# Two rewrites in the delta stage of a hybrid decoder step: the 64-row blocks of a triangular inverse, and how the query norms are summed

## The chip, the cores and the metric

The kernel runs on one core of one Trainium2 chip. A core has five engines that run side by side and meet through semaphores: TensorE (PE in the profile, with its weight loads shown apart as PEld), VectorE (DVE), ScalarE (ACT), GpSimd (POOL) and SyncE (SP), which issues most of the DMAs. TensorE writes its products to PSUM, and the other engines copy them from there to SBUF. The metric is the device time of one launch in microseconds (us); lower is better. Three timed runs of the kernel before gave 2085.28, 2088.38 and 2094.0 us, the median being 2088.38 us.

## The reference, cut to what matters

The program is one inference step of one decoder layer for a prompt of 1024 tokens and eight single-token samples: a combined input projection, a gated DeltaNet branch, a sliding-window attention branch, their mixture, a convolutional feed-forward part, and a last RMSNorm. The change lies in the DeltaNet branch for the prompt, which has 8 heads of width 128. Cut to that branch, per head, the reference computes:

```
q, k, v = split(silu(conv4(z)))                     # 1024 x 128 each
q = q * rsqrt(sum(q*q, -1) + EPS) * 128**-0.5        # l2 norm of each query row
k = k * rsqrt(sum(k*k, -1) + EPS)
m = strict_lower(beta * k @ k.T * gam)               # per chunk of rows
t_inv = inverse(eye + m)                             # unit lower triangular
u, w = t_inv @ (v * beta), t_inv @ (k * beta * exp(decay))
# then a scan over the chunks with the carried state S:
v_new = u - w @ S
o = q_dec @ S + a_intra @ v_new
S = S * last + k_dec.T @ v_new
out = o * rsqrt(mean(o*o, -1) + EPS) * w_norm * silu(gate)
```

The kernel computes the same thing with chunks of 128 rows instead of 64, so each head has 8 chunks and each chunk has a 128x128 inverse.

## The kernel before, in words

The 1032 tokens lie along the free axis and the channels along the 128 partitions. Every projection is a product in three passes (the high and low parts of weights and activations, lines L180, L181 and L182), over 8 blocks of the contracted width, for three token parts of 384, 384 and 264 columns. These projections make up most of TensorE's work in every stage.

The delta stage works head by head. `delta_project` makes K, Q and V of a head (projection, short convolution, SiLU). `delta_prepare` (L866) makes what does not depend on the running state: it transposes K on TensorE (L190) in two groups of four chunks, takes the squares of each chunk's rows with a running sum on ScalarE (L888), and scales the transposed K into `kd` (L890). It does the same transposes and squares for Q, where only the sums `n2` are used: they join the epsilon in the output norm of the scan (L972). One addition (L892) then adds an epsilon to all sums of K and Q together; `nk`, `c1`, the products K K and K Q (L906, L907), `A` (L908) and `U` (L910) follow, then V's transposes (`vn`, L918), and two loads of a row of decays into the tile `ed`, with which Q is multiplied (L922, L923).

`unit_inverse` (L990) inverts the unit triangular 128x128 matrices of the head's 8 chunks, by blocks that double in size: 16-row blocks by substitution on VectorE (L1019, L1020), then 32-row blocks (L1038, L1044), then 64-row blocks (L1056, L1061), and at the end the 128-row matrix from its two 64-row halves. This last step has two products per chunk, of 64x64 by 64x64. The first (L1070) uses array rows 0 to 63 and writes to partitions 64 to 127, so it uses array columns 64 to 127; ScalarE copies all eight chunks' results to `Zb` (L1071). The second (L1074) uses array rows 64 to 127 and columns 0 to 63; ScalarE copies its results into the inverse `W` (L1075). Both results live in PSUM tiles with the tag `tp`, of which there are two, shared with `delta_prepare`.

`delta_scan` (L931 and on) then walks through the 8 chunks with the state S. Each chunk is a chain across three engines: K times S (L947, TensorE), y (L948, VectorE), W times y (L950, TensorE), s (L952, ScalarE), kd times s (L954, TensorE), the new S (L963, VectorE). Every fourth chunk takes squares of the outputs on ScalarE (L969).

The order of the work is made when the program is built. `weave` (L1258) gives each stream of a head a priority: inverse first, scan next, then the next head's preparation, while the projections of later heads and of the two branch gates (L1294 and L1295 finish the gates) have the lowest priority and are the filler. A scheduler then writes one fixed order for each engine. On the chip every engine runs its list in that order: an instruction that waits for a semaphore holds up all that stand behind it on its engine. `issue_after(x)` asks the scheduler to put what is written inside the block behind instruction `x`; it ties those instructions of the block that are on the same engine as `x`.

## Time and profile before

| what | value |
|---|---|
| timed runs | 2085.28, 2088.38, 2094.0 us (median 2088.38) |
| span of the profiled execution, first to last instruction | 2084.4 us |
| the profiled execution's own time | not given apart from its span; the fastest timed run is 0.9 us above that span |
| TensorE busy | 2012.7 us, 97% |
| VectorE busy | 1347.8 us, 65% |
| ScalarE busy | 900.2 us, 43% |
| GpSimd busy | 520.2 us, 25% |
| delta stage of the prompt, from the timeline | about 412 to 1105 us |

The profile's groups by line give busy time, the mean of one instruction in ns, and the idle time of the engine just before it. In the timeline a row gives the start, the length, the engine, the line, and how many such instructions follow each other. A TensorE instruction's length includes its way through the array, and the next one starts before it ends; so what an instruction costs TensorE is read from the distance between two starts. A full fp32 product of this kernel shows as two matmul instructions (two passes), a transpose as one, and a pass of a projection as one. "Window" means a stretch of time from the span's start.

### The profile page before, as it was taken

What the parts mean: (1) busy time and instruction counts of PE and PEld (TensorE: products, weight loads), DVE (VectorE), ACT (ScalarE), POOL (GpSimd) and SP (SyncE); (2) the same over time, 40 slices, a digit from 0 to 9 for tenths busy, and PEclk for the clock granted to TensorE, in tenths of its full rate; (3) what the DMA queues carried; (4) which work ended last, traced back from release to release, by engine and by line L of the source; (5) the groups of instructions that cost most, each with busy time, mean ns of one, the idle gap of its engine ahead of it and who ended that gap; (6) DMA issues with size and microseconds to landing.
All of it is one profiled execution on the core that took longest, in us unless ns stands there. A gap on an engine that the chain in (4) does not pass through costs nothing.

```text
span 2084.4 us, 41297 instructions
## 1 busy us (share of the span) xinstructions
PE 2012.7 (97%) x16245; PEld 1910.2 (92%) x16245; DVE 1347.8 (65%) x2714; ACT 900.2 (43%) x2233; POOL 520.2 (25%) x594
## 2 busy tenths in 40 slices
PE   7999998999999999989989999999999999999897
PEld 4987877799999999989989999999999999999897
DVE  5755768473655647656544675578876776767756
ACT  4664545433344243432342542354444444534443
POOL 2000000121321221201111000005575466446421
PEclk9999999999999999999999999999999999999999
DMA  8256443331332322312275855323333333488862
GB/s 300 62 144 210 135 167 116 117 94 51 80 80 61 73 72 52 89 42 62 63 223 172 285 186 163 112 63 97 105 91 112 102 92 112 136 305 266 291 215 94
DMA packets 301887, 275.75 MB, mean 132 GB/s; under 512 B 59730, under 2 KB 248111, under 8 KB 301676
## 3 DMA queue, kind: packets, MB, share of 16 engines
q1 hardware_dynamic: 295642, 252.14, 39.6%
q0 software_dynamic: 5552, 20.37, 2.8%
q8 instruction: 127, 2.08, 0.4%
q14 instruction: 68, 0.56, 0.1%
q10 hardware_dynamic: 498, 0.61, 0.1%
HBM read 212.93 MB, written 62.51 MB: 132 GB/s over the span
## 4 chain that ended last, share of the span: by engine, by line
PE 83%; DVE 5%; DMA 5%; ACT 3%; issue 1%; SPq 1%; POOL 1%; DVEq 0%; POOLq 0%; ACTq 0%
PE mm L180 19%; PE mm L181 18%; PE mm L182 18%; PE wv L180 3%; PE wv L182 3%; PE wv L181 3%; PE wy L182 2%; PE wy L180 2%; PE wy L181 2%; PE pv L652 1%; PE pt L190 1%; PE tp L190 1%; DVE x L1472 1%; PE mm L264 1%; PE rc L954 1%
## 5 line engine op out<-in xcount | busy, mean ns | idle before, releaser
L180 PE MATMUL mm<-b1h,wh 128*128 128x384 f32 (+1 forms) x1520 | 496.9, 328 | 3.7 <-ACT gt L1294 1.6
L181 PE MATMUL mm<-b1l,wh 128*128 128x384 f32 (+1 forms) x1520 | 489.3, 323 | 0.0
L182 PE MATMUL mm<-b1h,wl 128*128 128x384 f32 (+1 forms) x1520 | 488.0, 323 | 0.3 <-DVE wl L130 0.3
L180 PEld LDWEIGHTS mm<-b1h,wh 128*128 128x128 f32 x1520 | 286.7, 189 | 12.4 <-issue 4.6
L181 PEld LDWEIGHTS mm<-b1l,wh 128*128 128x128 f32 x1520 | 287.1, 189 | 4.4 <-issue 3.1
L182 PEld LDWEIGHTS mm<-b1h,wl 128*128 128x128 f32 x1520 | 286.3, 189 | 3.9 <-issue 2.8
L129 ACT ACTIVATE wh<-raw 128x1024 fp32r<-128x1024 f32 x83 | 87.0, 1049 | 122.4 <-PE mm L181 70.2
L130 DVE TENSOR_TENSOR wl<-raw,wh 128x1024 fp32r<-128x1024 f32 x82 | 101.0, 1233 | 57.2 <-ACT wh L129 55.1
L181 PE MATMUL mm<-pk,w 128*128 128x260 f32 (+1 forms) x440 | 124.8, 284 | 1.1 <-DVE pk L130 1.1
L180 PE MATMUL mm<-pk,w 128*128 128x260 f32 (+1 forms) x440 | 124.8, 284 | 0.0
L182 PE MATMUL mm<-pk,w 128*128 128x260 f32 (+1 forms) x440 | 124.5, 283 | 0.0
L130 DVE TENSOR_TENSOR w<-ws,w 128x512 fp32r<-128x512 f32 x88 | 78.0, 886 | 36.9 <-ACT w L129 36.7
L1626 ACT COPY bml<-mm 128x256 f32<-128x256 f32 (+1 forms) x132 | 48.9, 371 | 100.6 <-PE mm L182 96.7
L180 PE MATMUL mm<-bmh,w 128*128 128x260 f32 (+1 forms) x320 | 90.3, 282 | 0.0
L182 PE MATMUL mm<-bmh,w 128*128 128x260 f32 (+1 forms) x320 | 90.1, 282 | 0.0
L1681 DVE SCALAR_TENSOR_TENSOR fa<-fz,fcw,fa 128x512 f32<-128x512 f32 x88 | 75.2, 874 | 18.2 <-ACT fa L1679 17.9
L180 PE MATMUL mm<-b2h,wh 128*128 128x384 f32 (+1 forms) x256 | 83.2, 328 | 2.9 <-ACT wh L129 2.8
L181 PEld LDWEIGHTS mm<-pk,w 128*128 128x128 f32 x440 | 83.2, 189 | 1.3 <-DVE pk L130 1.3
L181 PE MATMUL mm<-b2l,wh 128*128 128x384 f32 (+1 forms) x256 | 83.6, 327 | 0.4 <-DVE b2l L130 0.4
L180 PEld LDWEIGHTS mm<-pk,w 128*128 128x128 f32 x440 | 83.2, 189 | 0.2 <-ACT bml L1626 0.2
L182 PEld LDWEIGHTS mm<-pk,w 128*128 128x128 f32 x440 | 83.4, 190 | 0.0
L182 PE MATMUL mm<-b2h,wl 128*128 128x384 f32 (+1 forms) x256 | 82.8, 326 | 0.0
(645 smaller groups left out, 5886.2 us busy)
## 6 DMA issues: line engine op xcount, KB each, us to landing
raw<-in_w_in_dram SPq DMA_DIRECT2D x59, 512.0 KB
ws<-in_w_ffn_down_dram SPq DMA_DIRECT2D x55, 256.0 KB
raw<-xd SPq DMA_DIRECT2D x47, 258.0 KB
raw<-in_w_ffn_down_dram SPq DMA_DIRECT2D x47, 256.0 KB
raw<-in_w_ffn_gate_dram SPq DMA_DIRECT2D x22, 512.0 KB
raw<-in_w_ffn_up_dram SPq DMA_DIRECT2D x22, 512.0 KB
qst<-in_w_mod_dram SPq DMA_DIRECT2D x16, 512.0 KB
raw<-in_w_mod_dram SPq DMA_DIRECT2D x16, 512.0 KB
```

What stands on the lines that cost most here:

```text
L129: self.nc.scalar.activation(hi, x, AF.Copy)
L130: (eng or self.nc.vector).tensor_tensor(lo, x, hi.bitcast(F32), op=ALU.subtract)
L180: mm(ps, whi, xhi, start=first, stop=False, **kw)
L181: mm(ps, whi, xlo, start=False, stop=False, **kw)
L182: self.last_mm = mm(ps, wlo, xhi, start=False, stop=last, **kw).ins
L190: self.nc.tensor.transpose(out, in_, self.ident[:p, :p])
L264: nc.tensor.matmul(ps[32 * j:32 * j + 32], self.cT[:, k0 + j, :], ws[j // 2][:, j % 2, :], start=k0 == 0, stop=k0 > 0)
L652: nc.tensor.matmul(pv[64 * r:64 * r + 64], V[:, n - back, ch], ps[:, r::2, :], start=back == 0, stop=back == (n > 0))
L954: yield step(nc.tensor.matmul(ds, kd[:, n, :], s, start=True, stop=True))
L1472: nc.vector.scalar_tensor_tensor(x[:, :np_], ps[:, :np_], by[:, j, 8:9], x[:, :np_], op0=ALU.mult, op1=ALU.add)
L1626: self.last_copy = nc.scalar.copy(r[p, i], x[p])
L1681: nc.vector.scalar_tensor_tensor(ai[:, c:e], zi[:, j + c:j + e], col(j), ai[:, c:e], op0=ALU.mult, op1=ALU.add)
```

## The change

The change edits two functions.

In `delta_prepare`, Q is no longer transposed. K's two groups stay as they were, and the epsilon is now added to K's sums alone. For Q, ScalarE squares four chunks in one instruction into a tile `q2` that shares the buffer of `ed`; four products with 32 columns of ones as the stationary operand then sum over the partitions, each for 32 of the 128 tokens of a chunk and into its own 32 partitions, so that the sums of token block j stand in partitions 32j to 32j+31. VectorE turns the 32x32 blocks (L899 of the changed kernel), after which the sum of each token stands in its own partition, and adds the epsilon (L900). `q2`'s two groups, like the two loads of decays behind them, use the one buffer of `ed`.

In `unit_inverse`, the two products of the 64-row halves are cut into groups of four chunks. The written loop has three rounds: the first product of chunks 0 to 3; the first product of chunks 4 to 7 in turn with the second product of chunks 0 to 3; the second product of chunks 4 to 7. Each of the copies to `Zb` and to `W` is split in two. The rounds behind the first are written inside `issue_after(copied)`, where `copied` is ScalarE's copy and the block holds TensorE instructions. In the changed kernel's line numbers the first product is L1084, the second L1086, and the copies are L1088 and L1090; the scan's lines have moved down by nine (L950 is L959, and so on).

```diff
-        for a, src in ((0, K), (1, Q)):
-            for c0 in (0, 4):
-                tp = self.t(psum, [P, 4, P], "tp", bufs=2)
-                for c in range(4):
-                    self.transpose(tp[:, c, :], src[:, c0 + c, :])
-                junk = self.t(pool, [P, P], "osq", bufs=1)
-                for c in range(4):
-                    nc.scalar.activation(junk, tp[:, c, :], AF.Square, accum_out=n2[:, a, c0 + c:c0 + c + 1])
-                if a == 0:
-                    nc.vector.tensor_tensor(kd[:, c0:c0 + 4, :], tp, bc(self.edd[:, h, c0:c0 + 4], 2, P), op=ALU.mult)
-                yield
-        nc.vector.tensor_scalar_add(n2, n2, 4 * EPS)
+        for c0 in (0, 4):
+            tp = self.t(psum, [P, 4, P], "tp", bufs=2)
+            for c in range(4):
+                self.transpose(tp[:, c, :], K[:, c0 + c, :])
+            junk = self.t(pool, [P, P], "osq", bufs=1)
+            for c in range(4):
+                nc.scalar.activation(junk, tp[:, c, :], AF.Square, accum_out=n2[:, 0, c0 + c:c0 + c + 1])
+            nc.vector.tensor_tensor(kd[:, c0:c0 + 4, :], tp, bc(self.edd[:, h, c0:c0 + 4], 2, P), op=ALU.mult)
+            yield
+        nc.vector.tensor_scalar_add(n2[:, 0], n2[:, 0], 4 * EPS)
+        for c0 in (0, 4):
+            q2 = self.t(pool, [P, 4, P], "ed", bufs=1)
+            nc.scalar.activation(q2, Q[:, c0:c0 + 4, :], AF.Square)
+            sums = self.t(psum, [P, 4, 32], "tp", bufs=2)
+            for j in range(4):
+                r = slice(32 * j, 32 * j + 32)
+                nc.tensor.matmul(sums[r], self.ones[:, 0:32], q2[:, :, r], start=True, stop=True)
+            turned = self.t(pool, [P, 4, 32], "osq", bufs=1)
+            nc.vector.transpose(turned.rearrange("p n i -> p (n i)"), sums.rearrange("p n i -> p (n i)"))
+            nc.vector.tensor_scalar_add(n2[:, 1, c0:c0 + 4], turned[:, :, 0], 4 * EPS)
+            yield
...
         zp = self.t(psum, [P, NCH, 2, 32], "tp", bufs=2)
-        for n in range(NCH):
-            nc.tensor.matmul(zp[64:128, n], U64[:, n, :], TT[0:64, :, n, :], start=True, stop=True)
-        nc.scalar.copy(Zb, zp[64:128].rearrange("p n a i -> p n (a i)"))
         qp = self.t(psum, [64, NCH, 64], "tp", bufs=2)
-        for n in range(NCH):
-            nc.tensor.matmul(qp[:, n, :], Zb[:, n, :], W[64:128, n, 64:128], start=True, stop=True)
-        nc.scalar.copy(W[0:64, :, 64:128], qp)
+        copied = None
+        for c0 in (0, 4, 8):
+            with self.tc.issue_after(copied) if copied else nullcontext():
+                for n in range(c0, c0 + 4):
+                    if n < NCH:
+                        nc.tensor.matmul(zp[64:128, n], U64[:, n, :], TT[0:64, :, n, :], start=True, stop=True)
+                    if c0:
+                        nc.tensor.matmul(qp[:, n - 4, :], Zb[:, n - 4, :], W[64:128, n - 4, 64:128], start=True, stop=True)
+            if c0 < NCH:
+                copied = nc.scalar.copy(Zb[:, c0:c0 + 4], zp[64:128, c0:c0 + 4].rearrange("p n a i -> p n (a i)")).ins
+            if c0:
+                nc.scalar.copy(W[0:64, c0 - 4:c0, 64:128], qp[:, c0 - 4:c0])
```

The change also moves instructions, since the scheduler writes the whole order anew. Three places show it. In the rows a semaphore's name tells whom an instruction waits for (`Activation` is ScalarE, `DVE` VectorE, `Pool` GpSimd, `DMAHW` a transfer).

First, TensorE in head 0, at the end of the inverse. Before, the second products stand as one block of eight behind a block of projections:

```order
L180 MATMUL mm_5421<-b1h_10_148,wh_5417 128x384
L181 MATMUL mm_5421<-b1l_11_149,wh_5417 128x384
L1074 MATMUL tp_5149<-W_4535,UZ_4957 64x64 [waits Activation_49]
L1074 MATMUL tp_5149<-W_4535,UZ_4957 64x64 x7
L190 MATMUL tp_5848<-ident,K_4654 128x128 [waits PE_49]
```

Now, in the same head, the first products of chunks 4 to 7 and the second products of chunks 0 to 3 stand in turn:

```order
L181 MATMUL mm_5423<-b1l_11_149,wh_5419 128x384
L1084 MATMUL tp_5139<-MR_5019,UZ_4957 64x64 [waits Activation_49]
L1086 MATMUL tp_5140<-W_4535,UZ_4957 64x64 [waits PE_49]
L1084 MATMUL tp_5139<-MR_5019,UZ_4957 64x64
L1086 MATMUL tp_5140<-W_4535,UZ_4957 64x64
L1084 MATMUL tp_5139<-MR_5019,UZ_4957 64x64
L1086 MATMUL tp_5140<-W_4535,UZ_4957 64x64
L1084 MATMUL tp_5139<-MR_5019,UZ_4957 64x64
L1086 MATMUL tp_5140<-W_4535,UZ_4957 64x64
L182 MATMUL mm_5423<-b1h_10_148,wl_5420 128x384
```

The two kinds of products alternate here; the remaining four second products stand 23 rows further down.

Second, TensorE in head 5. Before, the scan's last two chunks and the block of second products stand like this:

```order
L954 MATMUL rc_9735<-s_9733,kd_8864 128x128 [waits Activation_49]
L958 MATMUL o_9698<-s_9733,A_8916 128x128
L182 MATMUL mm_10286<-b1h_12_150,wl_10255 128x384
L947 MATMUL rc_9742<-S_9739,K_7325 128x128 [waits DVE_49]
L957 MATMUL o_9698<-S_9739,Q_7326 128x128
L950 MATMUL rc_9745<-y_9741,W_4535 128x128 [waits DVE_49]
L954 MATMUL rc_9749<-s_9747,kd_8864 128x128 [waits Activation_49]
L958 MATMUL o_9698<-s_9747,A_8916 128x128
L1074 MATMUL tp_10183<-W_4535,UZ_9991 64x64 [waits PE_49,Activation_49]
L1074 MATMUL tp_10183<-W_4535,UZ_9991 64x64 x7
L190 MATMUL tp_10876<-ident,K_9341 128x128 x4
```

Now the first product's second half has gone ahead of these rows, and the second product stands in two groups:

```order
L963 MATMUL rc_9745<-s_9743,kd_8872 128x128 [waits Activation_49]
L967 MATMUL o_9708<-s_9743,A_8924 128x128
L956 MATMUL rc_9752<-S_9749,K_7331 128x128 [waits DVE_49]
L966 MATMUL o_9708<-S_9749,Q_7332 128x128
L959 MATMUL rc_9755<-y_9751,W_4535 128x128 [waits DVE_49]
L963 MATMUL rc_9759<-s_9757,kd_8872 128x128 [waits Activation_49]
L967 MATMUL o_9708<-s_9757,A_8924 128x128
L1086 MATMUL tp_10184<-W_4535,UZ_10001 64x64 [waits PE_49,Activation_49]
L1086 MATMUL tp_10184<-W_4535,UZ_10001 64x64 x3
L190 MATMUL tp_10888<-ident,K_9351 128x128 x4
L1086 MATMUL tp_10184<-W_4535,UZ_10001 64x64 [waits Activation_49]
L1086 MATMUL tp_10184<-W_4535,UZ_10001 64x64 x3
```

The products do not alternate in this head, nor in any of heads 1 to 7: each of the two products stands as two groups of four, and each second group waits for ScalarE. The wait of a second group is for the copy of the first group of the same product (L1088 or L1090).

Third, ScalarE in head 5, around the copies of the first product. Before, the one copy stands ahead of the gate's tanh (L858) and of the two convolution rows (L791):

```order
L129 ACTIVATE wh_10350<-raw_10348 128x1024 [waits DMAHW3_49,PE_49]
L780 COPY z_9534<-mm_9594 128x264 [waits PE_49]
L1071 COPY UZ_9991<-tp_10173 64x512 [waits PE_49]
L952 ACTIVATE s_9733<-rc_9731,c_1414_8912 128x128 [waits PE_49,Activation_49]
L858 ACTIVATE th_10311<-mm_10286 128x384 [waits PE_49]
L791 ACTIVATE z_9534<-v_1476_9343 128x512 [waits DVE_49,Activation_49,Pool_49]
L791 ACTIVATE z_9534<-v_1476_9343 128x512 [waits Activation_49]
```

Now both copies stand behind them:

```order
L1072 COPY w_1625_10178<-tp_10143 32x256 [waits PE_49]
L858 ACTIVATE th_10323<-mm_10298 128x384 [waits PE_49]
L791 ACTIVATE z_9544<-v_1486_9353 128x512 [waits DVE_49,Pool_49]
L791 ACTIVATE z_9544<-v_1486_9353 128x512 [waits Activation_49]
L1088 COPY UZ_10001<-tp_10183 64x256 [waits PE_49]
L961 ACTIVATE s_9743<-rc_9741,c_1424_8920 128x128 [waits PE_49]
L1088 COPY UZ_10001<-tp_10183 64x256 [waits PE_49]
```

The tanh and the convolution rows have moved ahead of the copies, and the scan's s (L952, now L961) stands between the two halves.

## The prediction

> **What bounds the kernel now.** I read the page's busy times first, then the chain that ended last, then the delta stage in windows.

> ```profile
> span 2084.4 us, 41297 instructions
> PE 2012.7 (97%) x16245; PEld 1910.2 (92%) x16245; DVE 1347.8 (65%) x2714; ACT 900.2 (43%) x2233; POOL 520.2 (25%) x594
> PE 83%; DVE 5%; DMA 5%; ACT 3%; issue 1%; SPq 1%; POOL 1%; DVEq 0%; POOLq 0%; ACTq 0%
> ...
> 585.00:670.00 85.00, 84.70 (x754) 82.17 (x753) 50.30 (x109) 30.27 (x85) 14.62 (x23) 1.00 0.27 67
> ...
> 840.00:925.00 85.00, 78.56 (x699) 75.03 (x697) 51.90 (x111) 31.66 (x97) 14.57 (x21) 0.94 0.23 61
> 925.00:1005.00 80.00, 79.59 (x711) 77.12 (x710) 48.65 (x107) 27.61 (x76) 11.42 (x19) 0.99 0.25 66
> 1005.00:1070.00 65.00, 61.99 (x606) 57.59 (x605) 38.05 (x100) 28.19 (x90) 11.66 (x17) 1.00 0.36 101
> 1070.00:1130.00 60.00, 52.77 (x378) 50.69 (x377) 26.50 (x52) 16.35 (x43) 7.91 (x10) 0.97 0.77 223
> ```

> A window's row gives its length, then the busy time of TensorE, its weight loads, VectorE, ScalarE and GpSimd. TensorE is the bound, and the chain runs through it for 83% of the span. In a middle head (585 to 670) it is idle for 0.3 us: there only TensorE's own work counts, and work taken from ScalarE is worth nothing. From 840 on, where the projections that fill gaps run short, it is idle for 6.4 + 0.4 + 3.0 + 7.2 = 17.1 us: there the length of the chain across engines counts too. So each edit has two prices: TensorE time in all heads, and chain time in heads 5 to 7.

> **The change part by part.**

> *Query sums, on TensorE.* Four transposes leave, four products of two passes each come, 16 times (8 heads, two groups).

> ```profile
> 600.43 0.34 PE L182 MATMUL mm<-b1h,wl 128*128 128x384 f32 x1
> 600.61 0.60 PE L190 MATMUL tp<-ident,v 128*128 128x128 f32 x4
> 600.97 0.42 PE L180 MATMUL mm<-b1h,wh 128*128 128x384 f32 x1
> 601.22 0.33 PE L181 MATMUL mm<-b1l,wh 128*128 128x384 f32 x1
> ...
> 210.26 0.34 PE L180 MATMUL mm<-b1h,wh 128*128 128x384 f32 x1
> 210.53 0.62 PE L264 MATMUL mm<-wmh,cTr 128*32 128x512 f32 x2
> 210.98 0.60 PE L264 MATMUL mm<-wmh,cTr 128*32 128x512 f32 x2
> 211.41 1.04 PE L264 MATMUL mm<-raw,cTr 128*32 128x512 f32 x8
> 212.38 0.44 PE L181 MATMUL mm<-b1l,wh 128*128 128x384 f32 x1
> 212.66 0.34 PE L182 MATMUL mm<-b1h,wl 128*128 128x384 f32 x1
> ...
> 656.74 0.38 PE L947 MATMUL rc<-S,K 128*128 128x128 f32 x2
> 656.96 0.39 PE L957 MATMUL o<-S,Q 128*128 128x128 f32 x2
> ```

> A projection pass costs 0.18 (600.43 to 600.61). Four transposes hold the engine for 0.36, and the pass behind them takes 0.25 instead of 0.18: 0.43 us go per group. For what comes, the modulation's product L264 has the same form: 128 rows, a strip of 32 columns, four strips in turn. Its eight last passes of 512 columns take 0.97 (211.41 to 212.38), a round of four 0.44 (210.53 to 210.98), so 0.11 per 512-column pass: four strips run at once. Our passes have 128 columns: two rounds of 0.11 are 0.22, the end costs 0.97 - 2 x 0.44 = 0.09, going to strips 0.09 (210.53 against 210.26 + 0.18) and back 0.10 (0.28 instead of 0.18). Together 0.50, so +0.07 per group and +1.1 us in all. Lower bound: changing there and back costs nothing, 0.31, -1.9 us. Upper bound: the passes run one behind another like a full product's, 0.22 for two (656.74 to 656.96), so 0.88 + 0.28 = 1.16, +11.7 us. I take +1.1, since L264 has the form itself.

> [...]

> ```profile
> 210.98 0.13 PEld L264 LDWEIGHTS mm<-raw,cTr 128*32 128x32 f32 x4 [0.30 <-issue]
> ```

> These four loads of 128 rows begin at 210.98, while passes begun at 210.53 last until 211.15. [...]

> *The 64-row blocks, on TensorE.*

> ```profile
> 663.74 0.34 PE L182 MATMUL mm<-b1h,wl 128*128 128x384 f32 x1
> 664.01 1.14 PE L1074 MATMUL tp<-W,UZ 64*64 64x64 f32 x16
> 665.08 0.65 PE L190 MATMUL tp<-ident,K 128*128 128x128 f32 x4
> ...
> 906.87 0.69 PE L1061 MATMUL tp<-T,tmp 32*32 32x32 f32 x32
> 907.49 0.39 PE L181 MATMUL mm<-b1l,wh 128*128 128x264 f32 x1
> ```

> Sixteen passes (eight products) take 1.07, and getting in costs 0.09 and out about 0.10: 1.26 per block, 2.52 per head. In turn on opposite quarters two products should take the time of one: L1061 alternates two tiles on different rows and columns, 32 passes in 0.62. No row has 64x64 tiles in turn, so 0.53 (all overlap) and 1.07 (none) bound eight products in turn. But the written order has them in turn in head 0 alone. The mark behind the copy ties only ScalarE's instructions and its block holds TensorE's, so it ties nothing; and the second half of each product waits for the copy of its own first half, from the same PSUM tile. In heads 1 to 7 the two halves of each product stand as groups of four, apart: four groups of 0.53 + 0.19 = 2.9 per head, +0.4, or +2.6 us. Head 0 has two such groups and one in turn: 2.2 with overlap, -0.35; 2.7 without, +0.2. I take -0.35. Sum +2.3; were all heads in turn with overlap it would be -2.8.

> *The new waits.* Each head now has two: TensorE waits for half a copy before it goes on with the same product. Before, only the one copy to `Zb` stood between them.

> ```profile
> 658.40 0.49 PE L950 MATMUL rc<-y,W 128*128 128x128 f32 x2
> 658.50 0.58 ACT L1071 COPY UZ<-tp 64x512 f32<-64x512 f32 x1 [0.35 <-PE tp L1070]
> 656.38 0.36 ACT L1063 COPY w<-tp 32x256 f32<-32x256 f32 x1 [3.51 <-PE tp L1061]
> 919.02 0.74 ACT L1065 COPY W<-tp 32x256 f32<-32x256 f32 x2
> 919.81 1.97 PE L1074 MATMUL tp<-W,UZ 64*64 64x64 f32 x16 [1.61 <-ACT W L1065]
> L129 ACT ACTIVATE wh<-raw 128x1024 fp32r<-128x1024 f32 x44 | 46.5, 1058 | 56.5 <-PE mm L181 45.4 <-DMA ed<-drow 4.6 <-DMA raw<-in_w_in_dram 3.5
> L791 ACT ACTIVATE z<-K 128x512 f32<-128x512 f32 x14 | 8.1, 624 | 9.9 <-DVE K L786 9.9
> ```

> A copy starts 0.10 after TensorE could go on (658.50 against 658.40), half of it takes 0.36 (256 columns), and TensorE starts 0.05 after its end (919.76 to 919.81): 0.51 must be covered. In the new order the cover is 20 rows or more in half of the 16 places, but in head 1 it is one projection pass and one product (0.40), in head 5 one product (0.22), and before the last four products of heads 4, 5 and 6 one group of transposes (0.36). Bare, that is 0.1 + 0.3 + 3 x 0.15 = 0.85 us. ScalarE, too, has a queue: in head 5 the first copy stands behind a tanh and two L791 (2 x 0.62), the W copies of heads 4 to 6 behind squares, that of head 6 also behind an L129 (1.06). I add 2 us for that: +2.9. Lower bound 0. Upper bound: the eight places with under 0.9 of cover each pay an L129 and the 0.51, 8 x 1.57 = +12.6. Behind the waiting instruction stand the scan's products and all filler.

> *ScalarE, VectorE, queues.*

> ```profile
> 665.77 0.28 ACT L888 ACTIVATE osq<-tp 128x128 f32<-128x128 f32 x1
> 666.17 0.28 ACT L888 ACTIVATE osq<-tp 128x128 f32<-128x128 f32 x1
> L1034 DVE STREAM_TRANSPOSE MR<-T 128x256 f32<-128x256 f32 x8 | 3.6, 446 | 18.4 <-DMA T<-wd 18.4
> L892 DVE TENSOR_SCALAR n<-n 128x16 f32<-128x16 f32 x8 | 1.4, 176 | 6.1 <-ACT osq L888 6.0
> ```

> ScalarE loses 64 squares at 0.40 (25.6 us), gains 16 of 512 columns at 0.62 (L791's; 10.0) and 2.2 us by splitting copies (16 x 2 x 0.36 - 16 x 0.58): -13 us. VectorE gains 16 turns (under L1034's 0.45) and 24 - 8 additions of 0.18: below +10 us on an engine at 65%. In heads 0 to 4 both are hidden behind projections (idle 0.3). In heads 5 to 7 K's norm no longer waits for Q's eight squares (3.2 us per head), and `U` comes earlier. Idle that this can win at the two borders 5 to 6 and 6 to 7 is about 1 us each: -2, bounds 0 and -4. The decay loads now stand back to back on SyncE's queue ahead of the inverse's first transfers, but they no longer wait there for the next head's buffer, so I cost them at 0; if their landing were late, the next inverse would start late, uncovered from head 5 on.

> *Sum:* +1.1 + 2.3 + 2.9 - 2.0 = +4.3 us on the profiled 2084.4, 2088.7. The span lies 4.0 below the runs' median of 2088.4; with the same difference the timed median would be 2092.7; I take 2092.

> **The rivals.** About 0.5% (10.4 us; 2077.9 and 2098.8) is what a measurement of this kernel can tell.

> *A, the waits decide (slower).* In-order TensorE stands behind ScalarE's queue. For: eight thin covers. Against: in the middle heads today's copies leave 0.3 us of idle. It would give +1.1 + 2.3 + 12.6 - 2 = +14, 2102. It decides from 1.1 us per thin place on (8 x 1.1 + 1.4 = 10).

> *B, relief wins (faster).* The shorter preparation takes half of the 17.1 us idle from 840 on, and waits cost nothing: -8.5 + 2.3 - 1.9 = -8, 2080. For: that idle lies where the norms stand. Against: most of it is the scan's and the transfers' own. For over 0.5% it must win 11 of the 17.

> *C, strips run one behind another.* +11.7 in place of +1.1: +15, 2103. Against: L264. [...]

> *D, nothing of it is seen:* the halves hide and the order's luck is nil, 2088.

> **How the numbers follow.** Forecast 0.56, A 0.14, B 0.15, C 0.04, D 0.11. Over 0.5% faster is under half of B, 0.07; slower is A, C, and none of the rest: 0.18; within 0.5% remains 0.75. The range: forecast with its luck of order (5 us either way), down to B and up to A: 2079 to 2104.

> **What would show it.** Right: the new sums' eight passes in 0.3 to 0.5 with the four strips begun within 0.1 us; L1084 and L1086 of head 0 taking about 0.5 for 16 passes, in heads 1 to 7 four blocks of 0.53; idle ahead of L1084 and L1086 "<-ACT" of 2 to 4 us in all; ScalarE 13 us less busy; idle from 840 on near 17 us. Wrong: strip passes 0.11 apart (C), over 9 us of such idle (A), idle after 840 below 9 (B), or a difference outside the delta stage.

## The result, and the profile after

The changed kernel took 2099.4 us (median of five runs, 2096.44 to 2102.78) against 2088.38 us (2085.28 to 2094.0): +11.0 us, a ratio of 1.0053 with a 95% interval of 1.0037 to 1.0069. It is slower beyond doubt, and the interval has the 0.5% mark inside it. The forecast was +4.3 us. The profiled execution shows:

```profile
span 2097.0 us, 41355 instructions
PE 2018.9 (96%) x16309; PEld 1906.6 (91%) x16309; DVE 1355.4 (65%) x2746; ACT 888.4 (42%) x2137; POOL 520.8 (25%) x594
```

ScalarE is 11.8 us less busy, as the change meant, and that buys nothing. The windows shown of before are now as follows; the third number from the end of a row is the granted clock of TensorE.

```profile
585.00:670.00 85.00, 85.00 (x764) 81.38 (x763) 53.47 (x115) 30.93 (x80) 15.27 (x24) 1.00 0.27 71
...
840.00:925.00 85.00, 80.06 (x716) 75.58 (x714) 51.71 (x115) 29.58 (x83) 14.15 (x22) 0.96 0.24 63
925.00:1005.00 80.00, 77.30 (x696) 73.51 (x696) 51.19 (x113) 29.16 (x80) 14.77 (x20) 0.96 0.24 60
1005.00:1070.00 65.00, 60.66 (x591) 56.49 (x589) 34.64 (x99) 23.03 (x70) 10.50 (x17) 0.97 0.31 85
1070.00:1130.00 60.00, 52.75 (x395) 50.04 (x396) 27.24 (x52) 23.58 (x59) 5.58 (x6) 0.97 0.71 207
```

The middle head is as full as before. From 840 on, the clock is under 1 in every window, where before it was 0.94, 0.99, 1.00 and 0.97. The last product of the scan comes 10.8 us later (1126.26 against 1115.47), but 2.6 of these are there before the stage begins. Its first rows are, of before and then of after:

```profile
412.89 1.03 PE L190 MATMUL tp<-ident,K 128*128 128x128 f32 x8
...
415.50 1.03 PE L190 MATMUL tp<-ident,K 128*128 128x128 f32 x8
```

This start lies between 411.2 and 418.3 us in the profiled executions of all kernels of this document, so it tells nothing of the change. The stage itself is 8.2 us longer, and another 1.8 us of the 12.6 between the two spans come behind it. TensorE's waits in the stage, after (what waits, for whom, us in total, times, longest):

```profile
PE rc L963 <- ACT s L961: 4.9, 4, 2.4
PE tp L1086 <- ACT W L1074: 3.2, 3, 1.6
PE rc L190 <- DVE vn L985: 2.4, 2, 1.4
PE tp L190 <- ACT W L1090: 1.6, 3, 0.6
...
PE tp L1086 <- ACT W L1090: 1.5, 2, 1.0
...
PE rc L959 <- DVE y L957: 1.3, 3, 0.7
...
PE tp L1084 <- ACT UZ L1088: 0.8, 2, 0.4
```

and of before:

```profile
PE rc L954 <- ACT s L952: 5.2, 7, 1.8
PE rc L950 <- DVE y L948: 3.3, 5, 1.6
...
PE tp L1074 <- ACT W L1065: 1.6, 1, 1.6
...
PE rc L190 <- DVE vn L976: 0.7, 1, 0.7
...
PE tp L190 <- ACT W L1075: 0.3, 1, 0.3
```

The waits for the two halves' copies (L1088, L1090) come to 0.8 + 1.5 + 1.6 = 3.9 us, where before there were 0.3. The scan's own waits for s and y came down meanwhile, from 5.2 + 3.3 = 8.5 to 4.9 + 1.3 = 6.2 us. The idle of TensorE from 412 to the end of the scan grows only by 2.8 us, from 19.5 to 22.2 (703.5 less 684.05 busy, 714.3 less 692.07).

### The profile page after: what moved, and what is told of

Read it like the earlier page. It is cut to its first block, busy times and chain, and to the rows that moved or that the text cites. A ratio compares the mean times of both kernels' runs of the same rounds, so it can differ in the third digit from the quotient of the medians.

```text
span 2097.0 us, 41355 instructions
## 1 busy us (share of the span) xinstructions
PE 2018.9 (96%) x16309; PEld 1906.6 (91%) x16309; DVE 1355.4 (65%) x2746; ACT 888.4 (42%) x2137; POOL 520.8 (25%) x594
## 4 chain that ended last, share of the span: by engine, by line
PE 75%; DMA 8%; DVE 8%; ACT 3%; issue 2%; SPq 1%; POOL 1%; DVEq 0%; POOLq 0%; ACTq 0%
PE mm L180 17%; PE mm L182 17%; PE mm L181 17%; PE wv L180 2%; PE wv L182 2%; PE wv L181 2%; PE pv L652 1%; PE wy L180 1%; PE wy L182 1%; PE wy L181 1%; DMA raw<-xd 1%; PE pt L190 1%; DMA raw<-in_w_swa_out_dram 1%; PE mm L264 1%; DMA ws<-in_w_ffn_down_dram 1%
## 5 line engine op out<-in xcount | busy, mean ns | idle before, releaser
L180 PE MATMUL mm<-b1h,wh 128*128 128x384 f32 (+1 forms) x1520 | 496.1, 328 | 6.7 <-DVE gt L1341 1.5
L181 PE MATMUL mm<-b1l,wh 128*128 128x384 f32 (+1 forms) x1520 | 489.0, 323 | 0.0
L182 PE MATMUL mm<-b1h,wl 128*128 128x384 f32 (+1 forms) x1520 | 487.9, 324 | 0.6 <-DVE wl L130 0.6
L180 PEld LDWEIGHTS mm<-b1h,wh 128*128 128x128 f32 x1520 | 286.4, 189 | 16.5 <-issue 4.8
L181 PEld LDWEIGHTS mm<-b1l,wh 128*128 128x128 f32 x1520 | 286.6, 189 | 5.3 <-issue 3.1
L182 PEld LDWEIGHTS mm<-b1h,wl 128*128 128x128 f32 x1520 | 285.8, 189 | 5.3 <-issue 3.0
L129 ACT ACTIVATE wh<-raw 128x1024 fp32r<-128x1024 f32 x83 | 87.1, 1049 | 124.3 <-PE mm L181 82.3
L181 PE MATMUL mm<-pk,w 128*128 128x260 f32 (+1 forms) x440 | 125.0, 284 | 1.1 <-DVE pk L130 1.1
L180 PE MATMUL mm<-pk,w 128*128 128x260 f32 (+1 forms) x440 | 125.0, 284 | 0.0
L182 PE MATMUL mm<-pk,w 128*128 128x260 f32 (+1 forms) x440 | 124.8, 284 | 0.0
L180 PE MATMUL mm<-bmh,w 128*128 128x260 f32 (+1 forms) x320 | 90.4, 282 | 0.0
L182 PE MATMUL mm<-bmh,w 128*128 128x260 f32 (+1 forms) x320 | 90.2, 282 | 0.0
L181 PEld LDWEIGHTS mm<-pk,w 128*128 128x128 f32 x440 | 83.5, 190 | 1.3 <-DVE pk L130 1.3
L180 PE MATMUL mm<-b2h,wh 128*128 128x384 f32 (+1 forms) x256 | 82.6, 325 | 2.0 <-ACT wh L129 1.7
L180 PEld LDWEIGHTS mm<-pk,w 128*128 128x128 f32 x440 | 83.5, 190 | 0.2 <-ACT bml L1641 0.2
L182 PEld LDWEIGHTS mm<-pk,w 128*128 128x128 f32 x440 | 83.7, 190 | 0.0
L181 PE MATMUL mm<-b2l,wh 128*128 128x384 f32 (+1 forms) x256 | 82.9, 324 | 0.4 <-DVE b2l L130 0.4
L182 PE MATMUL mm<-b2h,wl 128*128 128x384 f32 (+1 forms) x256 | 82.3, 324 | 0.0
```

The lines of the kernel that those rows point to most:

```text
L129: self.nc.scalar.activation(hi, x, AF.Copy)
L180: mm(ps, whi, xhi, start=first, stop=False, **kw)
L181: mm(ps, whi, xlo, start=False, stop=False, **kw)
L182: self.last_mm = mm(ps, wlo, xhi, start=False, stop=last, **kw).ins
```

## The experiments

Three theories stood at the start. By the first, the change costs what its parts cost TensorE, plus the waits of the halves. By the second, the norm part is the cause. By the third, any edit in this stage makes the scheduler write the order anew, and that costs by itself. Differences in this section are medians against the kernel before in the same set of runs; the interval is that of the ratio.

| kernel | against before, us | ratio (95%) | stage, us | idle | half-clock loss |
|---|---|---|---|---|---|
| before | 0 | 1 | 702.6 | 19.5 | 6.8 |
| the change | +11.0 | 1.0053 (1.0037 to 1.0069) | 710.8 | 22.2 | 10.2 |
| e1_norms | +17.8 | 1.0085 (1.0068 to 1.0101) | 720.3 | 27.6 | 18.7 |
| e2_halves | +13.3 | 1.0065 (1.0048 to 1.0082) | 712.0 | 25.3 | 13.6 |
| e3_kfirst | +7.2 | 1.0034 (1.0022 to 1.0047) | 706.4 | 24.3 | 10.3 |
| e4_in_turn | +22.6 | 1.0112 (1.0095 to 1.0128) | 720.6 | 30.7 | 18.8 |
| f_before_200 | +14.3 | 1.0070 (1.0050 to 1.0091) | 712.2 | 24.2 | 12.0 |
| f_before_300 | +11.8 | 1.0055 (1.0037 to 1.0073) | 711.7 | 22.8 | 15.4 |
| f_after_200 | +11.0 | 1.0056 (1.0038 to 1.0074) | 713.2 | 21.7 | 15.4 |
| f_after_300 | +8.4 | 1.0046 (1.0027 to 1.0065) | 710.1 | 20.9 | 12.0 |
| f_before_251 | -0.3 | 0.9998 (0.9986 to 1.0010) | 701.7 | 18.2 | 6.8 |
| f_after_251 | +12.9 | 1.0060 (1.0045 to 1.0075) | 710.2 | 20.5 | 10.2 |
| g_waits | +6.6 | 1.0032 (1.0018 to 1.0046) | 704.7 | 20.1 | 8.6 |
| h_tied_waits | +18.3 | 1.0080 (1.0062 to 1.0097) | 702.2 | 18.1 | 8.6 |

The stage runs from head 0's first transposes of K to the start of the scan's last product in the one profiled execution; idle is its length less TensorE's busy time; the loss is the sum of (1 - granted clock) x 4 us over windows of 4 us from 412 to 1140. The stages of before, f_before_251, g_waits and h_tied_waits have the same or nearly the same order and lie between 701.7 and 704.7 us, so one execution tells a stage to about 3 us. A profiled execution can lie some us off the median of its kernel (that of f_after_251 spans 2090.1 us, its median is 2098.75).

### The parts alone: e1_norms, e2_halves, e3_kfirst, e4_in_turn

**e1_norms** is the kernel before with only the diff's part in `delta_prepare`; **e2_halves** has only the part in `unit_inverse`. **e3_kfirst** is the kernel before with one addition split:

```diff
             for c0 in (0, 4):
                 ...
                 yield
-        nc.vector.tensor_scalar_add(n2, n2, 4 * EPS)
+            nc.vector.tensor_scalar_add(n2[:, a], n2[:, a], 4 * EPS)
```

**e4_in_turn** is the whole change, with the products really tied one behind another on TensorE:

```diff
+        last = None
         for c0 in (0, 4, 8):
-            with self.tc.issue_after(copied) if copied else nullcontext():
-                for n in range(c0, c0 + 4):
-                    if n < NCH:
-                        nc.tensor.matmul(zp[64:128, n], ...)
-                    if c0:
-                        nc.tensor.matmul(qp[:, n - 4, :], ...)
+            for n in range(c0, c0 + 4):
+                if c0:
+                    with self.tc.issue_after(last) if last else nullcontext():
+                        last = nc.tensor.matmul(qp[:, n - 4, :], ...).ins
+                if n < NCH:
+                    with self.tc.issue_after(last) if last else nullcontext():
+                        last = nc.tensor.matmul(zp[64:128, n], ...).ins
```

Expected of e1_norms:

> Only the norm part of the change; the inverse is that of the kernel before. Theory 1 (the change costs what its parts cost TensorE, plus the waits of the halves): eight strip passes hold TensorE 0.35 us plus about 0.10 at the border against 0.33 for four transposes, so about +2 us over 16 groups, less up to 2 us of relief in heads 5 to 7: 0 to +2 us on the kernel before, ratio 0.999 to 1.002. Theory 2 (the norm part is what makes the change slow, by the work behind ScalarE's square of 512 columns and the one buffer of ed): +6 to +11 us, ratio 1.003 to 1.005. Theory 3 (any edit of this stage moves the order and costs 3 to 5 us by itself): +3 to +5 us here, and about as much in every other run of this call.

Expected of e2_halves:

> Only the inverse part of the change; norms by transposes as before. In this kernel's order the products of opposite quarters stand in turn in six of eight heads (all but heads 1 and 6), not in one as in the changed kernel. Theory 1: in a head in turn TensorE is held 0.61 + 0.62 + 0.61 + one more change of tiling 0.19 against 2 x 1.08, about -0.1 us; in a head apart 4 x 0.61 + 0.38 more, about +0.6; sum about +0.5 us, and the waits of second groups, 2 to 5 us of idle: +2 to +6 us, ratio 1.001 to 1.003. Theory 2: 0 us. Theory 3: +3 to +5 us, with idle of TensorE outside the rows of the two products.

Expected of e3_kfirst:

> The kernel before with one edit: the epsilon is added to K's sums as soon as they are there, and to Q's after Q's squares, so that U no longer waits for Q's eight squares. Transposes, squares and the inverse are as before. Theory 1 (relief of the chain in heads 5 to 7, the gain that the prediction put at 2 us): -2 to 0 us, ratio 0.999 to 1.000. Theory 2: no change. Theory 3: +3 to +5 us.

Expected of e4_in_turn:

> The whole change, but the products of opposite quarters are tied one behind another on TensorE, so that they stand in turn in all eight heads: four first products, then eight products in turn, then four second products. Theory 1: TensorE is held 7 x (0.6 + 0.19) = 5.5 us less than in the changed kernel; against that, in heads 4 to 6 nothing stands between the groups, and two bare copies of about 0.5 us each are waited for: +3 us. It would be 2 to 3 us faster than the changed kernel, +7 to +9 us on the kernel before. Theory 2: like the changed kernel, +10 to +11 us, since the inverse isn't the cause. Theory 3: +3 to +11 us, and no relation to the number of groups in turn.

Measured: +17.8, +13.3, +7.2 and +22.6 us. The first theory falls: it had 0 to +2, +2 to +6, -2 to 0 and +7 to +9. The parts do not add up to the whole either: each alone is as slow as both together, or slower. So does the second theory, which had nothing for e2 and e3. The third has the sign of all four, but with +3 to +5 us (for e4 +3 to +11) it was too small for each. Whether the quarters' products stand in turn doesn't decide either: they do in no head of e1, in six heads of e2 and in all eight of e4, and all three are slower than the kernel before. The telling one is e3, which splits one small addition per head in two, leaves every product of TensorE as it was, and costs 7.2 us.

The tie of e4 does what the change wrote and did not get: in head 7 its sixteen passes in turn take 0.62 us. But it makes a wait of what was cover. These are its waits that grew most at the two products (L1084 is the second and L1087 the first product; L1089 is the copy to `Zb`, and L1076 is VectorE's turning of blocks ahead of the first product):

```profile
PE tp L1084 <- ACT UZ L1089: 4.3, 4, 1.8
PE tp L1087 <- DVE MR L1076: 3.0, 2, 1.8
```

In the changed kernel TensorE waited 0.8 us for this copy (at the first product's second group) and 0.2 for the turned blocks. With all products in turn, nothing is left to stand between a half and its copy in heads 4 to 6. That the fixed tie costs more than the loose order is thus no surprise; how much of the 22.6 us it explains, beside the order of the rest, was not separated.

### Nothing but the order: f_before_200, f_before_300, f_after_200, f_after_300

One number of the planner is changed, in the kernel before and in the changed one alike. No computing instruction is added, removed or altered (the profiles of before, f_before_200 and f_before_300 each count 16245 of TensorE, 2714 of VectorE, 2233 of ScalarE and 594 of GpSimd):

```diff
-                        streams.append((self.delta_prepare(pool, psum, h + 1), 250, 1))
+                        streams.append((self.delta_prepare(pool, psum, h + 1), 200, 1))
```

and the same with 300. Expected of f_before_200:

> The kernel before, with one number of the planner changed: the stream of the next head's preparation starts 200 instead of 250 steps behind the inverse. Every instruction is the same; only the order differs. Theory 3 (the fixed order of the kernel before fits the chip well, and an edit that makes the scheduler write it anew loses 4 to 12 us by idle time of TensorE and by the half clock that follows it): +3 to +12 us, with TensorE's work unchanged within 1 us, and idle and clock loss both higher. Theory 1 (what the parts cost decides, the order is worth under 2 us): -2 to +2 us.

Expected of f_before_300:

> The same with 300 in place of 250. Theory 3: +3 to +12 us. Theory 1: -2 to +2 us.

Expected of f_after_200:

> The changed kernel with the number 200 in place of 250; every instruction as in the changed kernel. Theory 3: anywhere from +4 us (its own work on TensorE with the order of before's quality) to +20 us on the kernel before, so more than 3 us from the changed kernel's +11 in at least one of the two runs. Theory 1: +9 to +13 us, like the changed kernel.

Expected of f_after_300:

> The changed kernel with the number 300 in place of 250. Theory 3: anywhere from +4 to +20 us on the kernel before. Theory 1: +9 to +13 us.

Measured: the kernel before, in two other orders, is 14.3 and 11.8 us slower, as much as the change or more. The changed kernel in these orders stands at +11.0 and +8.4. At the same number the changed kernel is thus 3.3 and 3.4 us *ahead* of the kernel before (2099.47 against 2102.74, 2096.79 against 2100.22), a difference that the intervals of some 4 us either way don't tell from none. Two expectations missed: +14.3 lies above the third theory's +12, and neither run of the changed kernel lies more than 3 us from its +11, as that theory had asked of at least one. The loss of the change is no more than what a new order costs without it.

Where it goes can be read from the stage's windows, of before:

```profile
412.00:840.00 428.00, 425.16 (x3774) 412.51 (x3773) 255.22 (x529) 162.95 (x474) 89.05 (x121) 1.00 0.28 74
840.00:1115.50 275.50, 258.89 (x2303) 246.76 (x2302) 159.96 (x355) 101.96 (x294) 40.84 (x60) 0.98 0.35 97
```

of f_before_300, with the stretch that cost most:

```profile
412.00:840.00 428.00, 422.08 (x3748) 410.00 (x3747) 252.58 (x523) 156.93 (x450) 78.78 (x118) 1.00 0.29 76
840.00:1127.80 287.80, 270.95 (x2350) 257.54 (x2350) 161.51 (x360) 108.34 (x319) 40.54 (x63) 0.95 0.34 94
...
910.00:917.50 7.50, 5.92 (x94) 5.52 (x95) 5.80 (x9) 1.84 (x4) 0.10 (x1) 1.00 0.27 72
917.50:938.50 21.00, 18.75 (x146) 15.57 (x145) 6.34 (x15) 11.58 (x45) 1.30 (x2) 0.51 0.06 23
```

These windows begin at 412 in both. From its own first rows (416.11 here) the stage of f_before_300 is 9.1 us longer with only 3.3 us more idle. TensorE's *busy* time grew by 5.8 us with the same instructions: for 21 us from 917.5 on, behind 1.6 us of idle, it ran at a granted clock of 0.51. The column of the loss has 8.6 us more than before; what of it falls into waits costs nothing. An idle stretch thus seems to have a second price, a stretch at half the clock behind it; that is tested below.

### A small change of the order: f_before_251, f_after_251

The number is 251 in place of 250. Expected of f_before_251:

> The kernel before with 251 in place of 250 in the planner: the same instructions, and under 2% of TensorE's rows elsewhere in the order. Theory 3 (what the order of before is worth is lost with a large reordering, not with a small one): 0 to +4 us. If the loss of 12 us at 200 and at 300 came with any change of the number, +10 us.

Expected of f_after_251:

> The changed kernel with 251: its third order. If the change costs nothing in itself and the loss is the order's, +6 to +14 us on the kernel before, in the band of the other orders of the changed kernel (+8 and +11). If a lucky order is found, 0 to +5 us.

Measured: -0.3 us (by the interval between -2.9 and +2.1) and +12.9 us. Touching the number costs nothing; it is the large reordering that costs. Four orders of the changed kernel lie at +8.4, +11.0, +11.0 and +12.9; they are not four independent draws, since those at 251 and 300 keep about 97% and 89% of its TensorE rows of this stage in sequence, and at 250 and 251 the changed kernel is behind the kernel before, where at 200 and 300 it is level. Two large reorderings of the kernel before, which keep about 67% and 61%, lie at +14.3 and +11.8. The order of the kernel before at 250, and its near copy at 251, stand 7 us and more below every other order of the stage that was run.

### The second price of a wait: g_waits, h_tied_waits

To test the half clock where nothing else changes, waits were put into the branch projections behind the delta stage, where TensorE is busy throughout and its clock is 1.00. The rows and order of the delta stage are those of before. ScalarE makes a chain of short reads of a tile just done, and a throwaway product ahead of the next tile (overwritten by that tile's first real product) waits for the chain:

```diff
+            if getattr(self, "held", None) is not None:
+                self.nc.tensor.matmul(ps[:, 0:32], self.ones, self.held, start=True, stop=True)
+                self.held = None
             for k in range(KC):
...
+        tiles, repeats = [0], {3: 2, 6: 5, 9: 9, 12: 14}
         def ya_out(t, ps):
+            tiles[0] += 1
+            m = repeats.get(tiles[0] - 6, 0)
+            if m:
+                self.held = self.t(pool2, [P, 32], "held", bufs=1)
+                for _ in range(m):
+                    nc.scalar.activation(self.held, ps[:, 0:32], AF.Copy, scale=0.0)
```

Expected of g_waits:

> The kernel before, its delta stage and that stage's order untouched; in the branch projections after it (about 1230 to 1280 us, where TensorE is busy 50.00 of 50 us at the full clock) four waits are put in: a throwaway product ahead of a tile waits for a chain of 2, 5, 9 and 14 short ScalarE rows that begin when the tile before is done. About 0.3 us each with 0.3 to start: waits of roughly 0.9, 1.8, 3 and 4.5 us. Clock theory (an idle stretch of 1.5 us and more is followed by a stretch of 3.4 us or a multiple of it at half clock, 1.7 us of loss each): the short wait costs only itself; the others show a granted clock near 0.5 for 3.4 to 7 us right behind them, together 5 to 10 us of loss beside about 9 us of idle, so +13 to +19 us in all. Rival (the half-clock stretches of the delta stage have another cause, power or the mix of products): the clock stays at 1.00 behind the waits, and the kernel is slower by the waits alone, +8 to +10 us.

Measured: +6.6 us, ratio 1.0032 (1.0018 to 1.0046), below both expectations. The run settles little, because three of the four waits never came about: the scheduler put another tile's products into them. The longest left 1.0 us of idle (between 1262.0 and 1268.8), with the clock at 1.00 behind it, and the shifted work met a wait that was 2.06 us in the kernel before and is 4.74 now:

```profile
1292.60:1296.00 3.40, 2.12 (x10) 0.50 0.32 99
```

Here a row has only the length, TensorE's busy time, the clock and the DMA. Behind the wait of 4.74 us the clock is 0.50; behind the 1.0 us of idle it is 1.00.

In **h_tied_waits** every later projection row stands behind the throwaway product, so that the waits are bare (the edit against g_waits):

```diff
-                self.nc.tensor.matmul(ps[:, 0:32], ...)
+                self.barrier = self.nc.tensor.matmul(ps[:, 0:32], ...).ins
...
-                with self.spaced():
+                with self.spaced(), self.tc.issue_after(self.barrier) if getattr(self, "barrier", None) else nullcontext():
...
-        tiles, repeats = [0], {3: 2, 6: 5, 9: 9, 12: 14}
+        tiles, repeats = [0], {2: 3, 5: 6, 8: 10, 11: 15}
```

Expected of h_tied_waits:

> As g_waits, where the scheduler had put other products into most of the inserted waits, but now all later projection rows stand behind the throwaway products, so the waits are bare: chains of 3, 6, 10 and 15 ScalarE rows of 0.21 us, so waits of about 0.9, 1.5, 2.4 and 3.4 us, some 12 us apart, in a stretch where TensorE is otherwise busy throughout at the full clock. The delta stage is that of the kernel before. Clock theory (in the delta stages of the profiles so far, stretches of half clock that cost 1.71 us or a multiple of it stand behind idle time of 1.4 us and more within 3.4 us, and behind none under that): no half clock behind the wait of 0.9, one stretch of 1.7 us loss behind that of 2.4 and one or two behind that of 3.4, and it is open for 1.5; 3.4 to 7 us of loss beside about 8 us of idle, +11 to +15 us. Rival (those stretches come from something else in the delta stage): the clock stays at 1.00 and the kernel is slower by the waits alone, +8 us.

Measured: +18.3 us, ratio 1.0080 (1.0062 to 1.0097). The four waits, from the timeline (start, length, and in brackets the idle time before):

```profile
1224.30 0.41 PE L159 MATMUL mm<-held,ones 128*128 128x32 f32 x2 [2.42 <-ACT held L1354]
1239.05 0.41 PE L159 MATMUL mm<-held,ones 128*128 128x32 f32 x2 [1.49 <-ACT held L1354]
1253.18 0.63 PE L159 MATMUL mm<-held,ones 128*128 128x32 f32 x2 [2.41 <-ACT held L1354]
1271.34 0.63 PE L159 MATMUL mm<-held,ones 128*128 128x32 f32 x2 [3.56 <-ACT held L1354]
```

and the clock around them:

```profile
1224.30:1227.70 3.40, 3.40 (x20) 0.67 0.21 58
1227.70:1231.10 3.40, 3.40 (x20) 0.83 0.00 0
...
1239.05:1242.45 3.40, 3.40 (x27) 1.00 0.22 63
...
1250.70:1253.10 2.40, 0.07 (x1) 0.93 0.00 0
1253.10:1256.50 3.40, 3.32 (x15) 0.50 0.22 58
1256.50:1259.90 3.40, 3.40 (x17) 0.55 0.00 0
...
1267.70:1271.30 3.60, 0.09 (x1) 0.80 0.06 18
1271.30:1274.70 3.40, 3.36 (x15) 0.50 0.00 0
1274.70:1278.10 3.40, 3.40 (x20) 0.71 0.00 0
```

The wait of 1.49 us leaves the clock at 1.00 (27 passes in the next 3.4 us). Behind that of 2.42 the two next windows lose 3.4 x (0.33 + 0.17) = 1.7 us. Behind those of 2.41 and 3.56 the loss is 0.17 + 1.70 + 1.53 = 3.4 and 0.72 + 1.70 + 0.99 = 3.4 us, of which 0.17 and 0.72 fall into the wait itself and cost nothing. Together 7.6 us beside 9.9 us of waits: 17.5 of the 18.3 us measured, where the rival had 9.9 by these waits. An idle stretch causes the half clock; it is nothing peculiar to the delta stage. The first wait was 2.42 where 0.9 was meant, so +18.3 lies above the +11 to +15 that were expected: it was the list of sizes that missed. Each loss is 1.7 us or twice that, that is 3.4 or 6.8 us at half clock, and 2.41 us of idle were enough for it. The 1.5 us of idle from which the clock theory of g_waits counted was the author's estimate; the bare wait of 1.49 us left the clock at 1.00.

The length of a wait isn't the whole condition either. The kernel before and f_before_251 have the same wait of 2.06 us behind the branch projections (two windows of before, then two of f_before_251; columns as above):

```profile
1280.80:1284.20 3.40, 1.64 (x14) 1.00 0.20 44
1284.20:1287.60 3.40, 3.10 (x26) 1.00 0.75 225
...
1283.20:1286.60 3.40, 1.34 (x11) 1.00 0.43 115
1286.60:1290.00 3.40, 3.40 (x19) 0.50 0.74 217
```

In the clock's records in the traces of before and after, each stretch between two changes lasts 3.41 us or a whole multiple of it, but for the last, which the end of the trace cuts: half clock for 3.41 us six times in before and four times in after, and for 6.83 us two and four times. So the changes lie on a grid of 3.41 us. The windows of before above lie on it, and in f_before_251 the half clock fills its second window, 1286.6 to 1290.0. In before the grid cuts the wait into 1.8 and 0.3 us, and the clock stays; in f_before_251 all of it lies in one window, and the next one has half the clock. In the traces of before and after, 1190 windows of the grid are at full clock. All 8 of them with more than 1.85 us of TensorE idle were followed by half clock, and none of the 1148 with less than 1.05 us; of the 34 in between, 8 were. (Idle is what the profile's busy time leaves.) So in these traces the idle within one window of the grid counts, and small waits in it add up; what decides between the two bounds stays open. How long the half clock then lasts was not settled: in after a window of it with 0.21 us of idle (928.06 to 931.47) was followed by another at half clock, while in before one with 0.48 us (891.71 to 895.13) was not, and in f_before_300 21 us stood at 0.51.

## Why the prediction was right and wrong

The range of 2079 to 2104 held the time, the direction was right, the bound was named rightly, and the new waits came out near their price. The likeliest time was 7.4 us too low, and that the range held was luck in part: the forecast with its 5 us for the order ends at 2097, and 2099.4 lies inside only because the range was drawn up to rival A, whose waits did not come.

*Query sums.* Predicted 0.50 per group against 0.43, +1.1 us in all. In the one group that stands between projection passes of 384 columns:

```profile
422.57 0.34 PE L182 MATMUL mm<-b1h,wl 128*128 128x384 f32 x1
422.84 0.43 PE L897 MATMUL tp<-ed,ones 128*32 128x128 f32 x8
423.19 0.45 PE L180 MATMUL mm<-b1h,wh 128*128 128x384 f32 x1
423.48 0.34 PE L181 MATMUL mm<-b1l,wh 128*128 128x384 f32 x1
```

It takes 423.48 - 422.57 - 2 x 0.175 = 0.56, so +0.13 per group, +2.1 us. The four strips run at once, eight passes in 0.35 where one behind another, at 0.11 each, they would take 0.88, and rival C is out.

*64-row blocks.* That head 0 alone would stand in turn, and heads 1 to 7 in groups of four, was so, and opposite quarters overlap fully:

```profile
496.70 0.27 PE L1084 MATMUL tp<-MR,UZ 64*64 64x64 f32 x1
496.71 0.27 PE L1086 MATMUL tp<-W,UZ 64*64 64x64 f32 x1
...
497.32 0.45 PE L182 MATMUL mm<-b1h,wl 128*128 128x384 f32 x1
```

Sixteen passes take 0.62 instead of 1.07. But a group of four products apart takes 0.60, not the 0.53 that half a block was put at, and with its borders 0.81 between projections, not 0.72. Four are 3.24 per head against 2 x 1.27, +0.7 rather than +0.4: up to +4.9 us in seven heads, less where a group stands beside other small products that pay for the border anyway. This term was mis-sized by about half. (By the stage's balance, 8.2 - 2.8 idle - 3.4 half clock, TensorE's own work grew by 2.0 us in all, beside the 3.4 forecast and up to 7.0 by these rows. Across the other kernels of the table this remainder lies between -5 and +3 us, since half clock inside a wait is counted too, so it is no exact sum.)

*New waits and relief.* Predicted +2.9 and -2.0. Measured: 3.6 us more for the halves' copies, and 2.8 us more of idle in all, so everything else together came down by only 0.8. The scan's waits for s and y gave 2.3 us back, but `vn` (the scan's normed output) is now waited for with 2.4 us instead of 0.7, and `W` (L1074, before L1065) with 3.2 instead of 1.6. So the relief was not seen on balance. ScalarE's waits ahead of the two products come to 3.2 + 1.5 + 0.8 = 5.5 us, above the sign of 2 to 4 and far below A's 9: rival A's eight places at 1.57 each did not come.

*What was left out.* Two steps. First, an idle stretch was priced at its own length. The windows quoted in the prediction had 0.94 and 0.97 in the column of the clock, and it passed over them: in the kernel before, 2.3 us of idle between 915.5 and 919 stood ahead of 7 us at half clock (length, TensorE's busy time, the clock and the DMA):

```profile
915.50:919.00 3.50, 1.20 (x6) 1.00 0.00 0
919.00:926.00 7.00, 6.05 (x34) 0.51 0.04 12
```

The change's halves meet `W`, their own copies, K's transposes and `vn` in a row, and the sum of small waits does it (0.64 + 1.39 = 2.0 us of idle from 1016.8 to 1020.2, then a clock of 0.50 to 1023.6):

```profile
1015.03 0.68 PE L1086 MATMUL tp<-W,UZ 64*64 64x64 f32 x8 [0.76 <-ACT W L1074]
...
1016.75 0.68 PE L1086 MATMUL tp<-W,UZ 64*64 64x64 f32 x8 [0.46 <-ACT W L1090]
1018.07 0.66 PE L190 MATMUL tp<-ident,K 128*128 128x128 f32 x4 [0.64 <-ACT W L1090]
1020.11 1.06 PE L190 MATMUL rc<-ident,vn 128*128 128x128 f32 x4 [1.39 <-DVE vn L985]
```

Four transposes take 0.66 at 1018.07, and four of the same size take 1.06 two us later. In the stage this loss went from 6.8 to 10.2 us, +3.4, with no term in the sum.

Second, and larger: the sum was made as if all other rows stayed where the trace of before has them. They don't, and the runs at 200 and 300 show that a new order alone costs what was measured for the change. The 5 us "luck of order" in the range was taken as even to both sides. All ten kernels with a largely rewritten order, the change among them, were slower, by 7 to 23 us (they keep between a third and three quarters of before's TensorE rows of this stage in sequence): the trace shown was that of an order that fits the chip better than any of these. What in that order does it was not settled. In the profiles of all ten the idle (20.5 to 30.7 us) and the half-clock loss (10.2 to 18.8 us) of the stage are above the 19.5 and 6.8 of before (and above the 18.1 to 20.1 and 6.8 to 8.6 of the four profiles with its order); which rows of the order bring them was not traced, and no order was found for the changed kernel that regains it. No run was faster than the kernel before by more than the noise.

## What to carry to other kernels

When a scheduler writes the order, run the kernel before in a few other orders first (one planner number, nothing else): that spread is what an edit of this size has to be compared with, and the edit is then judged at equal numbers, not against the one order that was kept. On an engine that is 97% busy, read the clock column next to the idle: in the traces of before and after, more than 1.85 us of idle within one window of the 3.41 us grid was followed each time by 3.41 or 6.83 us at a clock of 0.50, a loss of 1.7 or 3.4 us, so covering one of several small waits can be worth more than shortening work. When stages of two executions are compared, measure from the stage's own first row, since a fixed time can be some us off. A mark that ties instructions acts only if it ties what it is meant to: look at the order that comes out, and at what stands between a copy and its reader once the tie holds.
